# A sparse-attention layer on one core: the output projection's second column half waits for the compressed branch, and the last tile's left half goes first

## The chip, the cores and the metric

The kernel runs on 1 core of a Trainium2 chip. The core has a matrix engine (TensorE, PE in the rows, with its weight loads as PEld), three engines for element-wise work (VectorE or DVE, ScalarE or ACT, GpSimd or POOL) and SyncE (SP), which issues the transfers. Each engine works through its own queue in order, and the engines wait for each other on semaphores. The metric is the device time of the whole program in microseconds (us), as a median over runs. Before the change it is 470.14 us over 3 runs (467.9, 470.14 and 470.22).

## The reference

One layer (DEPTH = 1, so the retention mixer never runs) over 512 tokens of width 1024:

```python
u = rms_norm(h, pre_norm_gain)
q, kv, g, z = split_cols(u @ w_in, ...)       # 16 heads of 64, 4 key/value groups
o_cmp, p_cmp = nsa_compressed(q, kc, vc, table)   # 31 compressed blocks
o_slc = nsa_selected(q, k_s, v_s, sel, table)
o_win = nsa_window(q, k_w, v_w, table)
y = sum(gates * [o_cmp, o_slc, o_win] * silu(z))  # 512 x 1024
out = h + rms_norm(y @ w_out, post_norm_gain)
```

The change touches only the last line: the product with `w_out` (1024 x 1024), the norm over the 1024 columns of a token, the multiplication by the norm's weight, and the sum with `h`.

## The kernel before, in words

All products are float32 split in a high and a low part, so that one product is three matmuls (high by high, low by high, high by low). A weight tile arrives by DMA in one of three buffers `wr`; `split_raw` (L106 to L119) makes the high part on ACT (L113, one cast) and the low part on POOL (L118, two subtractions). A buffer is free for the next load when POOL has read it.

Attention runs over 28 units (group, kind, query tile). For each, `qk` makes scores (L591), a minimum on DVE (L603) and the exponential on ACT (L604); `pv`, one unit later, transposes 128x128 blocks on PE (L681), splits them on ACT (`pth`, L684) and DVE (`ptl`, L685), and multiplies by the values (L714, L715). The head outputs are gathered into `y` (L722 to L731) and split again (`split_y`, L802 and L803). For the last group the order of the query tiles is 0, 3, 2, 1, and tile 1 comes last.

Everything else on PE (projections of the coming groups, and at the end the output projection `wout`) is a generator `fill`, from which the loop at L948 to L965 pulls steps in between, as a running cost estimate `clock` says. A scheduler then orders each engine's queue; `tc.keep_in_program_order` pins single instructions.

`wout` works on four token tiles of 128 rows (`turn = [0, 3, 2, 1]`) and two column halves of 512. The inner dimension has four parts of 256 rows (one for each head group): parts 0 to 2 (`w`, with `yhl` of groups 0 to 2) can be multiplied early, part 3 (`w3`, with `y3`) only when the last group is done. Before the change:

- L839 to L849: for each column half, the three weight tiles are loaded, parts 0 to 2 are multiplied in a PSUM bank of the pair `pj`, and ACT copies the sum into `og` (L849). Tile 1's right half is left out here.
- L850 waits in program order for the compressed branch of group 3, then `w3` is loaded for both halves (L852, L853) and the norm's weight `gb`.
- L875 to L905: for each tile and half, part 3 is multiplied in a bank, DVE adds it to `og` (L892), ACT squares and sums (L894), POOL makes the factor `fss` (`rstd`, L88 and L90), POOL multiplies the left half by the norm's weight (L900) and DVE the right one (L901); one tile later `finish` (L871, DVE) makes `og * fss + x` in `xr`, and SP sends it out (L872). For the last tile, tile 1, parts 0 to 2 of the right half are multiplied first (`late`), then part 3 of the left half, then part 3 of the right half into `late`, from which ACT reads directly.

Of the kernel before, what the change touches and what calls it, by code (L numbers as in the profile page):

```python
# [11 lines left out]
F32 = mybir.dt.float32  # L12
F32R = mybir.dt.float32r
AF = mybir.ActivationFunctionType
ALU = mybir.AluOpType
# [4 lines left out]
S = 512  # L20
D = 1024
# [4 lines left out]
NT = S // 128  # L26
# [25 lines left out]
def nsa_layer(ctx: ExitStack, tc: tile.TileContext, x, pre_gain, post_gain, table, w_in, w_out,  # L52
              k_pos, k_w1, k_w2, v_pos, v_w1, v_w2, hot, hot_c, out):
    nc = tc.nc
    V, A, P, T, SP = nc.vector, nc.scalar, nc.gpsimd, nc.tensor, nc.sync
    x = x.rearrange("b s d -> (b s) d")
    out = out.rearrange("b s d -> (b s) d")
# [12 lines left out]
    pj = lambda: bank("pj", 2)  # L70
# [749 lines left out]
    def wout():  # L820
# [4 lines left out]
        def wo_tile(kp, c, home=None):  # L825
            raw = load_raw([((lambda raw: raw.rearrange("p (k a) c -> p k (a c)", k=2)),
                             w_out[kp * 256:(kp + 1) * 256, c * S:(c + 1) * S].rearrange("(k p) c -> p k c", p=128))])
            return [v.rearrange("p (k a) c -> p k (a c)", k=2) for v in split_raw(raw, 4, A, P, home)]

        def wo_mm(p, kp, t, a, b, first, last):  # L830
            ts = slice(t * 128, (t + 1) * 128)
            for kk in range(2):
                yh, yl = yhl[kp][0][:, kk, ts], yhl[kp][1][:, kk, ts]
                T.matmul(p, yh, a[:, kk], start=first and kk == 0, stop=False)  # L834
                T.matmul(p, yl, a[:, kk], start=False, stop=False)  # L835
                T.matmul(p, yh, b[:, kk], start=False, stop=last and kk == 1)  # L836
                yield 650

        for c in range(2):  # L839
            cs = slice(c * S, (c + 1) * S)  # L840
            w = [wo_tile(kp, c) for kp in range(3)]
            yield 0
            for pair in (turn[0:2], turn[2:4 - c]):
                ps_ = [pj() for _ in pair]
                for kp in range(3):
                    for p, t in zip(ps_, pair):
                        yield from wo_mm(p, kp, t, *w[kp], kp == 0, kp == 2)
                for p, t in zip(ps_, pair):
                    A.copy(og[t][:, cs], p)  # L849
        while (3, B_CMP) not in zdone:  # L850
            yield None
        w3 = [wo_tile(3, 0, [keep.tile([128, 4, 256], F32R, name="w3", tag="u", bufs=8) for _ in range(2)]),  # L852
              wo_tile(3, 1, [at.tile([128, 4, 256], F32R, name="w3", tag="zs", bufs=3) for _ in range(2)])]  # L853
        gb = []
# [2 lines left out]
            SP.dma_start(g_, dview(post_gain, i * S, [[0, 128], [1, S]]))  # L857
            gb.append(g_)
        yield 0
        xrs = []  # L860
        for i in range(NT):
            if i < 3:
                t = wp.tile([128, D], F32, name="xr", tag="wr", bufs=3)
                xrs.append([t[:, 0:S], t[:, S:D]])
            else:
                xrs.append([keep.tile([128, S], F32, name="xr", tag="q", bufs=8) for _ in range(2)])

        def finish(t, xr, ss):
            for i in range(2):
                hs = slice(i * S, (i + 1) * S)  # L870
                V.scalar_tensor_tensor(xr[i], og[t][:, hs], ss, xr[i], op0=ALU.mult, op1=ALU.add)  # L871
                SP.dma_start(out[t * 128:(t + 1) * 128, hs], xr[i])  # L872

        prev = None
        for j, t in enumerate(turn):  # L875
            if j == 3:
                late = pj()
                for kp in range(3):
                    yield from wo_mm(late, kp, turn[3], *w[kp], kp == 0, False)
            while len(ready) <= j:  # L880
                yield None
            assert ready[j] == t
            for i in range(2):
                SP.dma_start(xrs[j][i], x[t * 128:(t + 1) * 128, i * S:(i + 1) * S])
            os_ = [og[t][:, i * S:(i + 1) * S] for i in range(2)]
            for i in range(2):
                held = j == 3 and i == 1
                p = late if held else sb() if j >= 2 else pj()
                yield from wo_mm(p, 3, t, *w3[i], not held, True)
                src = p if held else os_[i]  # L890
                if not held:
                    V.tensor_tensor(os_[i], os_[i], p, op=ALU.add)  # L892
                junk = at.tile([128, S], F32, name="junk", tag="lc", bufs=1)
                A.activation(junk, src, AF.Square, scale=1.0 / 32, accum_out=sumsq[:, t, i:i + 1])  # L894
                if j == 3:
                    V.tensor_tensor(os_[i], src, gb[i], op=ALU.mult)
            ss = const.tile([128, 1], F32, name="fss", tag="fss", bufs=4)
            rstd(ss, sumsq[:, t, 0:1], sumsq[:, t, 1:2])
            if j < 3:
                P.tensor_tensor(os_[0], os_[0], gb[0], op=ALU.mult)  # L900
                V.tensor_tensor(os_[1], os_[1], gb[1], op=ALU.mult)  # L901
            if prev is not None:
                finish(*prev)
            prev = t, xrs[j], ss
        finish(*prev)  # L905

    def kproj(g0):
        alloc_kd(g0)
# [95 lines left out]
```

## Time and profile before

| what | value |
|---|---|
| median of 3 runs | 470.14 us |
| the profiled execution, whole | 469.62 us |
| its span from the first to the last instruction | 467.8 us |
| granted TensorE clock, mean | 0.997 |
| PE busy | 451.2 us (96%) |
| DVE busy | 331.6 us (71%) |
| ACT busy | 274.9 us (59%) |
| POOL busy | 188.5 us (40%) |

Times in the rows are from the start of the span. 1.82 us of the execution lie outside the span. A matmul of 512 columns is shown with about 0.4 us, since it is pipelined: the next one starts about 0.23 us after it when nothing is waited for. A bracket at the end of a row is the time that the engine stood idle before it, and what it waited for.

### The profile page before, as it was taken

The numbers are of one execution on the slowest core, as the hardware profiler recorded it, in microseconds if no ns is written. First come the engines' busy times: TensorE is split into PE (matmuls) and PEld (weight loads), VectorE is DVE, ScalarE is ACT, GpSimd is POOL, SyncE is SP. The second block draws the span as 40 slices with busy tenths as digits, with TensorE's granted clock in tenths as the row PEclk, the third lists the DMA queues.
The fourth block names the chain that finished last, engine by engine and source line by source line (L and its number), as shares of the span: only waits on it lengthen the run. The fifth ranks groups of instructions, "written<-read, shape, count | busy, mean of one in ns | idle before, by whom it ended". The sixth has DMA issues, their size and how long they took to land.

```text
span 467.8 us, 6927 instructions
## 1 busy us (share of the span) xinstructions
PE 451.2 (96%) x2330; PEld 374.9 (80%) x2330; DVE 331.6 (71%) x799; ACT 274.9 (59%) x643; POOL 188.5 (40%) x188
## 2 busy tenths in 40 slices
PE   4999999999999999999999999999999999999993
PEld 3897888878888888888888788888878888887872
DVE  5879843852767888768759777786895867466686
ACT  5712232543776677767756867567675666566631
POOL 3423644243134463351563515245433353366242
PEclk9999999999999999999999999999999999999998
DMA  8589375263111331511141413033070211214013
GB/s 274 162 82 248 116 212 157 74 198 89 47 45 54 105 85 22 166 45 47 45 113 46 127 54 91 1 100 103 3 220 17 79 48 43 90 48 156 25 45 135
DMA packets 45501, 44.63 MB, mean 95 GB/s; under 512 B 7751, under 2 KB 38471, under 8 KB 45466
## 3 DMA queue, kind: packets, MB, share of 16 engines
q1 hardware_dynamic: 44424, 44.00, 33.1%
q8 instruction: 18, 0.29, 0.3%
q10 hardware_dynamic: 1042, 0.20, 0.2%
q14 instruction: 17, 0.14, 0.1%
HBM read 41.99 MB, written 2.20 MB: 94 GB/s over the span
## 4 chain that ended last, share of the span: by engine, by line
PE 84%; DVE 7%; ACT 3%; DMA 2%; issue 2%; POOL 1%; SPq 0%; DVEq 0%; POOLq 0%; ACTq 0%
PE ps_pj L146 11%; PE ps_pj L148 11%; PE ps_pj L147 11%; PE ps_s L591 9%; PE ps_t L681 7%; PE ps_o L715 4%; PE ps_o L714 4%; PE ps_pj L247 2%; PE ps_pj L248 2%; PE ps_pj L249 2%; PE ps_pj L834 2%; PE ps_pj L835 2%; PE ps_pj L836 1%; PE ps_s L247 1%; DMA wr<-in_nsa_w_in_dram 1%
## 5 line engine op out<-in xcount | busy, mean ns | idle before, releaser
L118 POOL TENSOR_TENSOR wl<-wr,wh 128x512 fp32r<-128x512 f32 x94 | 122.9, 1327 | 139.5 <-ACT wh L113 123.1
L146 PE MATMUL ps_pj<-uh,wh 128*128 128x512 f32 x240 | 99.0, 412 | 0.0
L148 PE MATMUL ps_pj<-ul,wh 128*128 128x512 f32 x240 | 94.2, 393 | 0.0
L147 PE MATMUL ps_pj<-uh,wl 128*128 128x512 f32 x240 | 94.2, 392 | 0.0
L604 ACT ACTIVATE p<-p,nm 128x512 f32<-128x512 f32 (+3 forms) x128 | 71.6, 560 | 24.3 <-DVE nm L603 23.5
L685 DVE TENSOR_TENSOR ptl<-ps_t,pth 128x512 fp32r<-128x512 f32 x80 | 55.0, 688 | 28.9 <-ACT pth L684 28.4
L113 ACT CAST wh<-wr 128x1024 fp32r<-128x1024 f32 x47 | 49.2, 1047 | 44.6 <-DMA wr<-in_nsa_w_in_dram 24.8
L591 PE MATMUL ps_s<-kd,q 128*128 128x512 f32 (+5 forms) x256 | 63.9, 336 | 0.6 <-DVE zs L699 0.6
L684 ACT CAST pth<-ps_t 128x512 fp32r<-128x512 f32 x80 | 46.3, 580 | 29.0 <-PE ps_t L681 28.4
L148 PEld LDWEIGHTS ps_pj<-ul,wh 128*128 128x128 f32 x240 | 45.1, 188 | 10.1
L591 PEld LDWEIGHTS ps_s<-kd,q 128*128 128x128 f32 x256 | 43.8, 189 | 9.0 <-DVE zs L699 1.1
L146 PEld LDWEIGHTS ps_pj<-uh,wh 128*128 128x128 f32 x240 | 45.2, 188 | 6.1
L147 PEld LDWEIGHTS ps_pj<-uh,wl 128*128 128x128 f32 x240 | 45.3, 189 | 5.9
L603 DVE CUSTOM_DVE_ANT_0 p<-ps_s,bias 128x128 f32<-128x128 f32 (+3 forms) x80 | 34.6, 447 | 20.9 <-PE ps_s L591 20.7
L681 PE MATMUL ps_t<-ident,p 128*128 128x128 f32 x320 | 48.4, 272 | 0.0
L681 PEld LDWEIGHTS ps_t<-ident,p 128*128 128x128 f32 x320 | 39.7, 140 | 9.3
L714 PE MATMUL ps_o<-pth,vt 128*128 128x512 f32 x80 | 33.7, 421 | 0.4 <-ACT pth L684 0.4
L728 POOL TENSOR_TENSOR y<-otmp,zs 128x256 f32<-128x256 f32 x16 | 12.3, 772 | 51.5 <-DVE otmp L725 51.5
L603 DVE CUSTOM_DVE_ANT_1 p<-ps_s,bias 128x256 f32<-128x256 f32 (+2 forms) x48 | 26.3, 554 | 9.1 <-PE ps_s L591 8.6
L715 PE MATMUL ps_o<-ptl,vt 128*128 128x512 f32 x80 | 32.3, 404 | 0.4 <-DVE ptl L685 0.2
L730 POOL TENSOR_TENSOR otmp<-otmp,zs 128x256 f32<-128x256 f32 x15 | 11.1, 741 | 38.3 <-DVE otmp L725 38.3
L569 ACT ACTIVATE zs<-ps_pj 128x512 f32<-128x512 f32 x22 | 13.1, 596 | 19.5 <-PE ps_pj L148 19.4
(268 smaller groups left out, 899.6 us busy)
## 6 DMA issues: line engine op xcount, KB each, us to landing
wr<-in_nsa_w_in_dram SPq DMA_DIRECT2D x36, 512.0 KB
wr<-in_nsa_w_in_dram SPq DMA_DIRECT2D x16, 256.0 KB
bias<-toepd SPq DMA_DIRECT2D x16, 256.0 KB
wr<-in_nsa_w_out_dram SPq DMA_DIRECT2D x8, 512.0 KB
xt<-in_x_dram SPq DMA_DIRECT2D x4, 512.0 KB
wr<-in_nsa_cmp_k_w_dram SPq DMA_DIRECT2D x4, 512.0 KB
wr<-in_nsa_cmp_v_w_dram SPq DMA_DIRECT2D x4, 512.0 KB
xr<-in_x_dram SPq DMA_DIRECT2D x8, 256.0 KB
```

The costliest lines, as they stand in the source:

```text
L113: A.copy(h[:, 0:kn], raw[:, 0:kn])
L118: el.tensor_tensor(l[:, ks], raw[:, ks], h[:, ks].bitcast(F32), op=ALU.subtract)
L146: T.matmul(p, a, rh, start=k == 0, stop=False)
L147: T.matmul(p, b, rh, start=False, stop=False)
L148: T.matmul(p, a, rl, start=False, stop=k == KT - 1)
L591: T.matmul(po, qs[h][:, qt * 128:(qt + 1) * 128], kds[h // R][:, i, c0:c0 + n], start=i == 0, stop=i == 1)
L603: V.tensor_tensor_reduce(pd, src, bi, 1.0, BIG, ALU.add, ALU.min, st["nm"][:, hh:hh + 1])
L604: A.activation(po, po, AF.Exp, bias=st["nm"][:, hh:hh + 1], scale=-1.0, accum_out=st["rs"][:, hh:hh + 1])
L681: T.transpose(tp[:, hh * 128:(hh + 1) * 128], st["p"][hh][:, c:c + 128], ident)
L685: V.tensor_tensor(pl, tp, ph.bitcast(F32), op=ALU.subtract)
L714: T.matmul(acc, v, ph, start=j == 0, stop=False)
L715: T.matmul(acc, v, pl, start=False, stop=j == qt)
```

## The change

- The three weight tiles of the second column half are asked for after the wait for the compressed branch, together with `w3`, so their products stand later in program order.
- Tile 0's right half is not copied into `og` any more. Its bank stays open (`held`) until part 3 is added in the same bank, and ACT and DVE read the sum there.
- The product with the norm's weight is on DVE for both halves (L922); POOL's L900 is gone.
- For tile 1, part 3 of the left half is multiplied before the eighteen matmuls of parts 0 to 2 of the right half, and tile 2's finishing steps stand on DVE after the left half's product, pinned in program order. Its products go to a new tile `og3`.
- `xr` is allocated inside the loop; its loads are the same.

```diff
-        for c in range(2):
-            cs = slice(c * S, (c + 1) * S)
-            w = [wo_tile(kp, c) for kp in range(3)]
-            yield 0
-            for pair in (turn[0:2], turn[2:4 - c]):
-                ps_ = [pj() for _ in pair]
-                for kp in range(3):
-                    for p, t in zip(ps_, pair):
-                        yield from wo_mm(p, kp, t, *w[kp], kp == 0, kp == 2)
-                for p, t in zip(ps_, pair):
-                    A.copy(og[t][:, cs], p)
+        def half(t, c):
+            return og[t][:, c * S:(c + 1) * S]
+
+        def partial(w, c, ts):
+            ps_ = [pj() for _ in ts]
+            for kp in range(3):
+                for p, t in zip(ps_, ts):
+                    yield from wo_mm(p, kp, t, *w[kp], kp == 0, kp == 2 and (c, t) != (1, turn[0]))
+            for p, t in zip(ps_, ts):
+                if (c, t) == (1, turn[0]):
+                    held.append(p)
+                else:
+                    A.copy(half(t, c), p)
+
+        held = []
+        w = [wo_tile(kp, 0) for kp in range(3)]
+        yield 0
+        yield from partial(w, 0, turn[0:2])
+        yield from partial(w, 0, turn[2:4])
         while (3, B_CMP) not in zdone:
             yield None
+        w = [wo_tile(kp, 1) for kp in range(3)]
...
+        def last(i):
+            return tc.keep_in_program_order(i)
+
+        def finish(t, xr, ss, i):
+            a = V.scalar_tensor_tensor(xr[i], g3[i] if t == turn[3] else half(t, i), ss, xr[i], op0=ALU.mult, op1=ALU.add)
+            if t in turn[2:]:
+                last(a)
+            SP.dma_start(out[t * 128:(t + 1) * 128, i * S:(i + 1) * S], xr[i])
...
-            if j == 3:
-                late = pj()
-                for kp in range(3):
-                    yield from wo_mm(late, kp, turn[3], *w[kp], kp == 0, False)
+            if j < 3:
+                if j == 0:
+                    yield from partial(w, 1, turn[0:2])
+                if j == 1:
+                    yield from partial(w, 1, turn[2:3])
...
+                whole = i == 1 and j in (0, 3)
+                if whole and j == 3:
+                    held.append(pj())
+                    for kp in range(3):
+                        yield from wo_mm(held[-1], kp, t, *w[kp], kp == 0, False)
+                p = held.pop(0) if whole else sb() if j >= 2 else pj()
+                yield from wo_mm(p, 3, t, *w3[i], not whole, True)
+                if not whole:
+                    a = V.tensor_tensor(half(t, i), half(t, i), p, op=ALU.add)
...
                 if j == 3:
-                    V.tensor_tensor(os_[i], src, gb[i], op=ALU.mult)
+                    g3.append(at.tile([128, S], F32, name="og3", tag="p", bufs=8))
+                    last(V.tensor_tensor(g3[i], src[i], gb[i], op=ALU.mult))
+                    if i == 0:
+                        finish(*prev, 0)
+                        finish(*prev, 1)
             rstd(ss, sumsq[:, t, 0:1], sumsq[:, t, 1:2])
             if j < 3:
-                P.tensor_tensor(os_[0], os_[0], gb[0], op=ALU.mult)
-                V.tensor_tensor(os_[1], os_[1], gb[1], op=ALU.mult)
+                for i in range(2):
+                    V.tensor_tensor(half(t, i), src[i], gb[i], op=ALU.mult)
...
```

ACT's queue where the weights for part 3 are cast, before. `w3_4917` belongs to the right half and to the second of the two loads (`wr_4919`), `w3_4910` to the left half and the first load (`wr_4912`); `pth_4698` and `pth_4722` are the casts that the attention of the unit before last waits for.

```order
L849 COPY og_4409<-ps_pj_4539 128x512
L802 CAST y30_4689<-y_4184 128x2x128
L113 CAST w3_4917<-wr_4919 128x1024
L684 CAST pth_4698<-ps_t_4693 128x512
L604 ACTIVATE p_4684,rs_4588<-p_4684,nm_4587 128x384
L113 CAST w3_4910<-wr_4912 128x1024
L684 CAST pth_4722<-ps_t_4717 128x512
```

The same place now. `w3_4694` is the first load (`wr_4696`), `w3_4701` the second (`wr_4703`).

```order
L851 COPY og_4409<-ps_pj_4539 128x512
L802 CAST y30_4660<-y_4184 128x2x128
L604 ACTIVATE p_4655,rs_4588<-p_4655,nm_4587 128x384
L684 CAST pth_4669<-ps_t_4664 128x512
L113 CAST w3_4694<-wr_4696 128x1024
L113 CAST w3_4701<-wr_4703 128x1024
L684 CAST pth_4740<-ps_t_4735 128x512
```

The exponential and one cast of the attention moved ahead of both casts of `w3`, and these two changed places. SP's queue keeps its order of loads; the one that is cast second now is also the one that is loaded second. On PE the two matmuls L591 and the four transposes L681 that feed this exponential and this cast moved up past six matmuls of the output projection, and on DVE the minimum L603 moved up past L803.

DVE's queue at the end of the program, before. Tile 3 is `og_4411`, tile 2 is `og_4410`, tile 1, the last, is `og_4409`.

```order
L871 SCALAR_TENSOR_TENSOR xr_4929<-og_4411,fss_4982,xr_4929 128x512 x2
L901 TENSOR_TENSOR og_4410<-og_4410,pgain_4926 128x512
L871 SCALAR_TENSOR_TENSOR xr_4930<-og_4410,fss_5013,xr_4930 128x512 x2
L892 TENSOR_TENSOR og_4409<-og_4409,ps_s_5043 128x512
L896 TENSOR_TENSOR og_4409<-og_4409,pgain_4924 128x512
L896 TENSOR_TENSOR og_4409<-ps_pj_5022,pgain_4926 128x512
L871 SCALAR_TENSOR_TENSOR xr_4931<-og_4409,fss_5063,xr_4931 128x512
L871 SCALAR_TENSOR_TENSOR xr_4932<-og_4409,fss_5063,xr_4932 128x512
```

The same place now.

```order
L922 TENSOR_TENSOR og_4410<-og_4410,pgain_4708 128x512
L874 SCALAR_TENSOR_TENSOR xr_4953<-og_4411,fss_4956,xr_4953 128x512
L922 TENSOR_TENSOR og_4410<-og_4410,pgain_4710 128x512
L907 TENSOR_TENSOR og_4409<-og_4409,ps_s_5022 128x512
L915 TENSOR_TENSOR og3_5032<-og_4409,pgain_4708 128x512
L874 SCALAR_TENSOR_TENSOR xr_4985<-og_4410,fss_4988,xr_4985 128x512 x2
L915 TENSOR_TENSOR og3_5065<-ps_pj_5038,pgain_4710 128x512
L874 SCALAR_TENSOR_TENSOR xr_5017<-og3_5032,fss_5021,xr_5017 128x512
L874 SCALAR_TENSOR_TENSOR xr_5018<-og3_5065,fss_5021,xr_5018 128x512
```

The last tile's left half is added (L892, now L907) and multiplied ahead of tile 2's two finishing steps instead of behind them, and left-half products stand here that were POOL's.

DVE's queue where the last `y` is made, now (tile 0 is `og_4408`; L730, L731 and L803 make tile 1's `y` and its low part).

```order
L922 TENSOR_TENSOR og_4408<-ps_pj_4712,pgain_4710 128x512
L730 TENSOR_TENSOR otmp_4909<-otmp_4909,zs_4228 128x256
L874 SCALAR_TENSOR_TENSOR xr_4869<-og_4408,fss_4872,xr_4869 128x512
L731 TENSOR_TENSOR y_4184<-y_4184,otmp_4909 128x2x128
L874 SCALAR_TENSOR_TENSOR xr_4869<-og_4408,fss_4872,xr_4869 128x512
L803 TENSOR_TENSOR y31_4661<-y_4184,y30_4660 128x2x128
```

Before, L730, L731 and L803 followed each other here; now tile 0's product and its two finishing steps, which wait for POOL's `fss_4872`, stand between them.

## Rows read from the trace of the kernel before

**Rows 1.** The page's busy times of the engines.

```profile
PE 451.2 (96%) x2330; PEld 374.9 (80%) x2330; DVE 331.6 (71%) x799; ACT 274.9 (59%) x643; POOL 188.5 (40%) x188
```

**Rows 2.** Stretches: length, busy of PE, PEld, DVE, ACT, POOL, clock, DMA, GB/s.

```profile
417.40:419.60 2.20, 2.20 (x12) 1.85 (x11) 1.21 (x3) 1.41 (x2) 1.30 (x2) 1.00 0.58 218
...
425.69:429.89 4.20, 3.47 (x21) 2.51 (x20) 3.79 (x7) 2.85 (x6) 4.20 (x4) 1.00 0.47 156
453.40:460.40 7.00, 7.00 (x31) 5.43 (x29) 7.00 (x11) 2.17 (x6) 4.01 (x5) 1.00 0.40 150
```

**Rows 3.** ACT in order of time: start, duration, instruction, [idle before, releaser].

```profile
422.40 0.41 ACT L802 CAST y<-y 128x256 fp32r<-128x256 f32 x1
424.49 1.05 ACT L113 CAST w<-wr 128x1024 fp32r<-128x1024 f32 x1 [1.68 <-DMA wr<-in_nsa_w_out_dram]
425.44 0.58 ACT L684 CAST pth<-ps_t 128x512 fp32r<-128x512 f32 x1
425.92 0.62 ACT L604 ACTIVATE p<-p,nm 128x384 f32<-128x384 f32 x1
...
427.47 1.07 ACT L684 CAST pth<-ps_t 128x512 fp32r<-128x512 f32 x2
430.17 0.59 ACT L684 CAST pth<-ps_t 128x512 fp32r<-128x512 f32 x1 [1.63 <-PE ps_t L681]
```

**Rows 4.** PE in order of time in the same stretch.

```profile
425.69 0.60 PE L681 MATMUL ps_t<-ident,p 128*128 128x128 f32 x4
...
426.81 0.50 PE L715 MATMUL ps_o<-ptl,vt 128*128 128x512 f32 x1 [0.22 <-DVE ptl L685]
...
429.54 0.60 PE L681 MATMUL ps_t<-ident,p 128*128 128x128 f32 x4
429.89 0.48 PE L834 MATMUL ps_pj<-wh,yhl 128*128 128x512 f32 x1
```

**Rows 5.** DVE in order of time in the same stretch.

```profile
421.19 0.69 DVE L787 TENSOR_TENSOR y<-y,ctmp 128x512 f32<-128x512 f32 x1
...
426.06 0.69 DVE L685 TENSOR_TENSOR ptl<-ps_t,pth 128x512 fp32r<-128x512 f32 x1 [1.91 <-ACT pth L684]
...
426.88 1.55 DVE L650 TENSOR_TENSOR f<-f,gate 128x256 f32<-128x256 f32 x1
428.35 0.68 DVE L685 TENSOR_TENSOR ptl<-ps_t,pth 128x512 fp32r<-128x512 f32 x1
```

**Rows 6.** All engines in order of time, the end of the program.

```profile
460.01 0.39 PE L836 MATMUL ps_pj<-w,y 128*128 128x512 f32 x1
460.23 0.67 DVE L892 TENSOR_TENSOR og<-og,ps_s 128x512 f32<-128x512 f32 x1
...
460.99 0.63 ACT L894 ACTIVATE junk<-og 128x512 f32<-128x512 f32 x1 [4.12 <-DVE og L892]
...
461.75 0.60 ACT L894 ACTIVATE junk<-ps_pj 128x512 f32<-128x512 f32 x1
...
462.24 0.19 ACT L894 ACTIVATION_READ_ACCUMULATOR junk<-ps_pj 128x1 f32 x1
...
463.51 1.42 DVE L871 SCALAR_TENSOR_TENSOR xr<-og,fss,xr 128x512 f32<-128x512 f32 x2 [0.35 <-POOL fss L90]
```

**Rows 7.** Tile `og` from 440 to 468: duration ns min/median/max, first and last start.

```profile
L871 DVE SCALAR_TENSOR_TENSOR xr<-og,fss,xr x8: 739/746/1772, 451.2 to 464.2; 128x512 f32<-128x512 f32 x8
L900 POOL TENSOR_TENSOR og<-og,pgain x3: 1285/1289/1293, 448.6 to 455.9; 128x512 f32<-128x512 f32 x3
L901 DVE TENSOR_TENSOR og<-og,pgain x3: 679/680/685, 450.1 to 458.3; 128x512 f32<-128x512 f32 x3
```

**Rows 8.** DVE and POOL in order of time, where tiles are finished.

```profile
451.17 1.28 POOL L900 TENSOR_TENSOR og<-og,pgain 128x512 f32<-128x512 f32 x1
451.23 1.77 DVE L871 SCALAR_TENSOR_TENSOR xr<-og,fss,xr 128x512 f32<-128x512 f32 x1 [0.46 <-POOL fss L90]
...
455.98 2.39 DVE L871 SCALAR_TENSOR_TENSOR xr<-og,fss,xr 128x512 f32<-128x512 f32 x2
```

More of the change, by code (lines that the diff above doesn't have):

```diff
@@ L859, in wout @@
         yield 0
[L860 to L874, printed above, removed]
-        for j, t in enumerate(turn):
-            if j == 3:
-                late = pj()
-                for kp in range(3):
-                    yield from wo_mm(late, kp, turn[3], *w[kp], kp == 0, False)
+        def last(i):
[5 more added lines that the diff above has]
+            SP.dma_start(out[t * 128:(t + 1) * 128, i * S:(i + 1) * S], xr[i])
+        prev, g3 = None, []
+        for j, t in enumerate(turn):
+            if j < 3:
[3 more added lines that the diff above has]
+                    yield from partial(w, 1, turn[2:3])
             while len(ready) <= j:
@@ L882, in wout @@
             assert ready[j] == t
+            if j < 3:
+                x_ = wp.tile([128, D], F32, name="xr", tag="wr", bufs=3)
+                xr = [x_[:, 0:S], x_[:, S:D]]
+            else:
+                xr = [keep.tile([128, S], F32, name="xr", tag="q", bufs=8) for _ in range(2)]
             for i in range(2):
-                SP.dma_start(xrs[j][i], x[t * 128:(t + 1) * 128, i * S:(i + 1) * S])
-            os_ = [og[t][:, i * S:(i + 1) * S] for i in range(2)]
+                SP.dma_start(xr[i], x[t * 128:(t + 1) * 128, i * S:(i + 1) * S])
@@ L886, in wout @@
+            ss = const.tile([128, 1], F32, name="fss", tag="fss", bufs=4)
+            src = []
             for i in range(2):
[L887 to L892, printed above, removed]
+                whole = i == 1 and j in (0, 3)
[7 more added lines that the diff above has]
+                    a = V.tensor_tensor(half(t, i), half(t, i), p, op=ALU.add)
+                    if j == 3:
+                        last(a)
+                src.append(p if whole else half(t, i))
@@ L893, in wout @@
                 junk = at.tile([128, S], F32, name="junk", tag="lc", bufs=1)
-                A.activation(junk, src, AF.Square, scale=1.0 / 32, accum_out=sumsq[:, t, i:i + 1])
+                A.activation(junk, src[i], AF.Square, scale=1.0 / 32, accum_out=sumsq[:, t, i:i + 1])
                 if j == 3:
-                    V.tensor_tensor(os_[i], src, gb[i], op=ALU.mult)
-            ss = const.tile([128, 1], F32, name="fss", tag="fss", bufs=4)
+                    g3.append(at.tile([128, S], F32, name="og3", tag="p", bufs=8))
[3 more added lines that the diff above has]
+                        finish(*prev, 1)
@@ L898, in wout @@
             rstd(ss, sumsq[:, t, 0:1], sumsq[:, t, 1:2])
             if j < 3:
-                P.tensor_tensor(os_[0], os_[0], gb[0], op=ALU.mult)
-                V.tensor_tensor(os_[1], os_[1], gb[1], op=ALU.mult)
[L902 to L905, printed above, removed]
+                for i in range(2):
+                    V.tensor_tensor(half(t, i), src[i], gb[i], op=ALU.mult)
+                if prev is not None:
+                    for i in range(2):
+                        finish(*prev, i)
@@ L907, in kproj @@
+            prev = t, xr, ss
+        for i in range(2):
+            finish(*prev, i)
     def kproj(g0):
```

## The prediction

> **What bounds the kernel now.** The page's busy times come first: PE is busy for 451.2 of the 467.8 us of the span, the next engine, DVE, for 331.6 [rows 1]. So a change of order pays in two places only: where PE stands still while work is left, and in the tail, after PE's last matmul. The number of matmuls is the same before and after, and their clock is 1.00 in every stretch shown with matmuls in it [rows 2], so PE's own work is not a term. I then read the timeline for these two places.
>
> The first is 425.69 to 429.89, the one stretch near the change where PE is busy for only 3.47 of 4.20 us [rows 2]. ACT shows why: after L802 (422.40, 0.41 long) it stood 1.68 us for the transfer of a `w3` tile and cast it at 424.49. Behind that in its queue were the attention's cast L684, which started at 425.44, and the exponential L604 [rows 3]. DVE's L685 had to wait for the first of them until 426.06 [rows 5], and PE's L715 for that until 426.81 [rows 4]. A second round of the same ended with DVE's L685 at 428.35 + 0.68 = 429.03 [rows 5], and the next matmul of the output projection came at 429.89 [rows 4].
>
> The second place is the tail. PE's last matmul starts at 460.01 and ends at 460.40. But DVE was in tile 2's finishing steps and added the left half of tile 1 only at 460.23; ACT squared this half at 460.99 and the right half, complete in PSUM since 460.40, only at 461.75. Its sum was read by 462.24 + 0.19 = 462.43, and DVE's finishing steps began at 463.51 [rows 6]. The span ends 467.80 - 463.51 = 4.29 us after that: two steps of 1.42 us together, the last transfer and the program's end.
>
> **The change part by part.**
>
> *ACT's order at the `w3` casts.* In the changed queue the exponential and one L684 stand ahead of both `w3` casts. I follow the queue with before's durations. L604 needs DVE's minimum, which now comes directly after L787, at 421.19 + 0.69 = 421.88 [rows 5]; the matmuls for it moved up past six others, so it is ready at about 422.5. ACT is free at 422.81 (L802). L604: 0.62, to 423.43; L684: 0.48 to the next start (425.44 to 425.92 [rows 3]), 423.91. The first `w3` cast takes 0.95 to the next start (424.49 to 425.44 [rows 3]), 424.86. Its load is there: the DMA engines moved 218 GB/s in 417.40 to 419.60 [rows 2], 480 KB, nearly all of one 512 KB tile. The second cast needs the second load, which landed at 424.49 in the trace and stands at the same place of SP's queue, behind the same POOL step; it is there with 0.37 us to spare. The cast ends its slot at 425.81. The next L684 waits for PE's transposes, unmoved at 425.69 + 0.60 = 426.29, and starts 0.03 after them, as at 430.17 after 429.54 + 0.60 [rows 3, 4]: 426.32. So ACT is no longer late. DVE's L685 follows 0.62 after such a cast starts (425.44 to 426.06) and takes 0.69: it ends at 427.63. In the trace the L685 at this place of the program ended at 429.03, after which PE reached the output projection 0.86 us later. **PE gains 429.03 - 427.63 = 1.40 us.**
>
> Bounds: if the transfer or the minimum came late, up to all of it goes, 0. The most is what PE lost there: with 12 transposes at 0.35 for four (429.54 to 429.89), four matmuls of 0.23, and 0.4 for two short groups, 4.20 us hold some 2.4 us of work, so 1.8 us. I take 1.40. Part of DVE's delay in the trace is its L650 at 426.88, which took 1.55 us beside POOL's steps [rows 5]; now it stands earlier, and even if it takes 1.55 there, the L685 behind it is done before PE asks for it at 426.3.
>
> *The same gain further on.* PE is in its own order after 429.89 and DVE, ACT and POOL follow it, so the 1.40 us stay, if nothing new makes PE wait. One place is near: the right half of tile 3 goes into the bank that ACT must first copy out (tile 2's right half). That copy stands on ACT behind a cast of the last `y`, which waits for DVE's L731, which now stands behind a finishing step of tile 0, which waits for POOL's factor. Following these queues from 1.40 us earlier, with ACT's extra square of 0.73, I get the bank free at about 447.8, when PE wants it at 447.7. A wait of this kind costs about 0.2 us. Before, PE had one of that size at the same place for DVE's L892. So net 0; the bounds are -0.2 and +1.4, the latter if a finishing step takes its longest, 1.77 in place of 0.74 [rows 7], and the factor 0.4 more.
>
> *Left half first, and finishing steps moved.* Tile 1's left half is complete eighteen matmuls earlier and is added, squared and multiplied before PE's end; at PE's end E only the right half is left. ACT's square starts 0.04 after E, the sum is read 462.43 - 461.75 = 0.68 later, and the finishing steps come 463.51 - 462.43 = 1.08 after that [rows 6]: E + 1.80. The trace had 463.51 - 460.40 = E + 3.11. **The tail gains 1.31 us.** Its cover is DVE: the left half, two products and tile 2's finishing must be done by then. By the same walk DVE ends tile 2's steps at about 458.2; with E = 459.0 the last product may start as late as E + 1.1, so there are about 1.9 us to spare. If that cover is gone, each us beyond it costs one.
>
> *Products on DVE.* Three of 0.68 on DVE in place of three of 1.29 on POOL, and one L892 of 0.67 less: 1.37 us more work on DVE. In 453.40 to 460.40 DVE was busy all 7.00 us [rows 2], so this is not obviously free. But that time holds blocked steps: a finishing step took 1.77 at 451.23 while POOL ran L900 at 451.17, and the pair at 455.98 took 2.39, against 0.74 for one [rows 7, 8]. That is 1.03 + 0.91 = 1.94 us that goes if L900 does it. I cost the products at 0, hidden behind PE's matmuls up to E; bounds 0 and +1.37.
>
> The Trainium skill, Perfetto Trace Analysis, section Optimizing Scalar/DVE Operations, speaks against this part: it says that work may be moved off VectorE, even to GpSimd, where VectorE is saturated, and adds that between these two a move might not help, since they share an SBUF read port. By its first half the sum would lose the 1.37 us; by the second, which the 1.77 beside L900 fits, it would not. I go by the rows.
>
> *The rest at nothing.* Tile 0's right half is no longer copied by ACT (about 0.6 us, hidden by PE either way). `xr`'s loads and the new tile `og3` add no instruction; SP's queue keeps its order of loads and stores.
>
> **Sum.** 1.40 + 0 + 1.31 = 2.7 us off the profiled execution's 469.62: 466.9. That execution is 0.5 us below the median of 470.14, inside the spread of 467.9 to 470.22; I say 467.0.
>
> **Rivals.**
>
> *PE gains nothing.* Its wait comes back a few us later, or the second load arrives over 0.9 us later than 424.49. For it: ACT has two casts in a row now, 2 x 0.95 us ahead of an L684. Against: the queues give room. Time: 469.62 - 1.31 = 468.3.
>
> *The bank.* Tile 0's finishing steps hold up ACT's copy, and PE waits 1.4 us at tile 3. For it: steps of 1.77 are in the trace. Against: POOL has no long step left there. Time: 469.62 - 2.7 + 1.4 = 468.3.
>
> *DVE becomes the bound, and the kernel slower.* The place is DVE's queue from 453.40 to PE's end, full in the trace. If the long finishing steps do not come from L900 but stay, the queue gets 1.37 us longer and the last finishing steps move by that: 469.62 + 1.37 = 471.0. This is what the rule on a saturated VectorE amounts to here. It decides once DVE ends tile 2's second step more than 1.9 + 2.7 us later than I reckon. Against it: blocked steps are only those beside L900.
>
> *No change.* The two gains were bounded by something else that ends at the same time, such as the stores; 469.6. Against: the last store is issued after the last step.
>
> **How the numbers follow.** My forecast 0.58, with its own range 465.8 to 467.8 (PE's gain up to 1.8 and the 0.2 of the old wait; or 0.9 less); no gain on PE 0.20; the bank 0.12; slower 0.06; none 0.04. The range reaches both cases at 468.3 with 1 us for the spread of runs: 465.2 to 469.4. About 0.5%, 2.35 us, can be told from no change. The forecast lies only 0.35 beyond it, so a good fifth of its chance falls within; of the two cases at 468.3 a fifth falls beyond. That gives 0.46 + 0.07 = 0.53 faster, 0.42 the same and 0.05 slower.
>
> **What would show it.** On ACT, a `w3` cast at 424 to 425 with no 1.68 us wait before it, and the exponential before 423.5. On PE, the matmuls after the stretch at 428.5 and the last one ending near 459.0. After it, ACT's square at once, the finishing steps 1.8 us later, and none of them over 0.8 us. I am wrong if PE ends at 460 or later, if a matmul of tile 3 waits for ACT's copy by over half a us, or if DVE is still in tile 2's steps when ACT squares.

## The result, and the profile after

The changed kernel takes 467.0 us (median of 8 runs, 465.29 to 468.0); the kernel before took 469.6 us in runs beside it. The ratio is 0.9944, 95% interval 0.9925 to 0.9963: 2.6 us, or 0.56%, faster. The prediction said 467.0. The profiled execution took 466.85 us with a span of 465.0 (before 469.62 and 467.8).

The page's busy times, against [rows 1], hardly differ; the span is shorter because the gaps are.

```profile
PE 450.9 (97%) x2330; PEld 375.3 (81%) x2330; DVE 330.6 (71%) x801; ACT 274.3 (59%) x642; POOL 184.7 (40%) x185
```

The first place is the stretch of [rows 2]. From the four transposes at 425.69 to the next matmul of the output projection took 4.20 us, 3.47 of them busy. It now takes 428.45 - 425.58 = 2.87 us, and PE is busy throughout (columns as in [rows 2]). The second line is the end of the program up to PE's last matmul; DVE, full there before, now has 0.62 us to spare.

```profile
425.69:428.50 2.81, 2.81 (x22) 2.41 (x20) 1.53 (x3) 1.17 (x2) 2.81 (x3) 1.00 0.53 187
453.40:458.85 5.45, 5.45 (x24) 4.16 (x22) 4.83 (x8) 1.45 (x4) 1.60 (x2) 1.00 0.32 123
```

ACT in order of time answers to [rows 3]. The exponential L604 and a cast L684 stand ahead of both `w3` casts (L113), which follow each other with no wait for a transfer. The next L684 waits for PE's transposes, not PE for it.

```profile
422.60 0.61 ACT L604 ACTIVATE p<-p,nm 128x384 f32<-128x384 f32 x1
...
423.21 0.57 ACT L684 CAST pth<-ps_t 128x512 fp32r<-128x512 f32 x1
423.68 2.01 ACT L113 CAST w<-wr 128x1024 fp32r<-128x1024 f32 x2
426.27 0.59 ACT L684 CAST pth<-ps_t 128x512 fp32r<-128x512 f32 x1 [0.58 <-PE ps_t L681]
427.12 0.59 ACT L684 CAST pth<-ps_t 128x512 fp32r<-128x512 f32 x1 [0.27 <-PE ps_t L681]
```

The tail, all engines in order of time, answers to [rows 6]. When PE's last matmul ends at 458.46 + 0.39 = 458.85, ACT squares the right half 0.10 us later, with no other square ahead of it. The finishing steps start at 460.72.

```profile
456.86 1.41 DVE L874 SCALAR_TENSOR_TENSOR xr<-og,fss,xr 128x512 f32<-128x512 f32 x2
...
458.46 0.39 PE L836 MATMUL ps_pj<-w,y 128*128 128x512 f32 x1
458.95 0.60 ACT L912 ACTIVATE junk<-ps_pj 128x512 f32<-128x512 f32 x1 [1.92 <-PE ps_pj L836]
459.44 0.19 ACT L912 ACTIVATION_READ_ACCUMULATOR junk<-ps_pj 128x1 f32 x1
459.67 0.69 DVE L915 TENSOR_TENSOR og<-ps_pj,pgain 128x512 f32<-128x512 f32 x1 [1.40 <-ACT junk L912]
...
460.72 1.42 DVE L874 SCALAR_TENSOR_TENSOR xr<-og,fss,xr 128x512 f32<-128x512 f32 x2 [0.35 <-POOL fss L90]
```

By the durations of tile `og` (minimum, median and maximum in ns), no finishing step is stretched any more; the longest in [rows 7] was 1772.

```profile
L874 DVE SCALAR_TENSOR_TENSOR xr<-og,fss,xr x8: 743/746/753, 445.4 to 461.4; 128x512 f32<-128x512 f32 x8
```

To compare profiles, I measure from one common event. PE's last L782, a matmul of the compressed branch, starts at 419.57 us before and at 419.46 after, ahead of the change's first effect on PE's order (420.85 after). In the profiles below it lies anywhere from 418.36 to 420.91. From its start to the start of PE's last matmul tells what PE gained; from that matmul's end, 0.39 later, to the first of the two final finishing steps is the tail.

```
kernel                        L782 to the   tail   L782 to the   by the trace   by the timed
                              last matmul           final step   vs before us   ratio us
before                           40.44      3.11      43.94          -              -
after                            39.00      1.87      41.26        -2.68          -2.6
left half first alone            41.93      1.86      44.18        +0.24          -0.2
order alone                      39.12      3.11      42.62        -1.32          -1.6
after, products on POOL          38.99      1.86      41.24        -2.70          -2.8
after, tile 0 copied             39.28      1.86      41.53        -2.41          -2.8
before, w3 loads swapped         39.41      3.09      42.89        -1.05          -0.8
after, six more on DVE           38.99      3.67      43.05        -0.89          -1.1
left half, products on DVE       40.41      1.86      42.66        -1.28          -1.1
order and left half              40.64      1.86      42.89        -1.05          -1.4
left half, six ahead             40.98      1.86      43.23        -0.71          -0.9
order, left half, six ahead      39.49      1.85      41.73        -2.21          -2.2
```

All of the change's 2.68 us is thus 1.44 on PE and 1.24 in the tail. The last column is the ratio less one, times the 469.6 to 470.0 us of the kernel before; its intervals are given with each run and reach 0.7 to 1.1 us to either side.

### The profile page after: what moved, and what is told of

The parts are those of the page before. It is cut to its first block, busy times and chain, and to the rows that moved or that the text cites. A ratio compares the mean times of both kernels' runs of the same rounds, so it can differ in the third digit from the quotient of the medians.

```text
span 465.0 us, 6924 instructions
## 1 busy us (share of the span) xinstructions
PE 450.9 (97%) x2330; PEld 375.3 (81%) x2330; DVE 330.6 (71%) x801; ACT 274.3 (59%) x642; POOL 184.7 (40%) x185
## 4 chain that ended last, share of the span: by engine, by line
PE 89%; DVE 4%; ACT 3%; issue 2%; POOL 1%; DVEq 0%; POOLq 0%; ACTq 0%
PE ps_pj L146 11%; PE ps_pj L148 11%; PE ps_pj L147 11%; PE ps_s L591 9%; PE ps_t L681 7%; PE ps_o L715 4%; PE ps_o L714 4%; PE ps_pj L834 3%; PE ps_pj L835 3%; PE ps_pj L836 3%; PE ps_s L247 2%; PE ps_s L248 2%; PE ps_s L249 2%; PE ps_pj L247 2%; PE ps_pj L248 1%
## 5 line engine op out<-in xcount | busy, mean ns | idle before, releaser
L604 ACT ACTIVATE p<-p,nm 128x512 f32<-128x512 f32 (+3 forms) x128 | 71.6, 560 | 24.3 <-DVE nm L603 23.5
L113 ACT CAST wh<-wr 128x1024 fp32r<-128x1024 f32 x47 | 49.2, 1047 | 43.5 <-DMA wr<-in_nsa_w_in_dram 20.1
L591 PE MATMUL ps_s<-kd,q 128*128 128x512 f32 (+5 forms) x256 | 63.9, 336 | 0.7 <-DVE zs L699 0.6
L684 ACT CAST pth<-ps_t 128x512 fp32r<-128x512 f32 x80 | 46.4, 580 | 29.3 <-PE ps_t L681 28.7
L591 PEld LDWEIGHTS ps_s<-kd,q 128*128 128x128 f32 x256 | 43.9, 189 | 9.0 <-DVE zs L699 1.2
L603 DVE CUSTOM_DVE_ANT_0 p<-ps_s,bias 128x128 f32<-128x128 f32 (+3 forms) x80 | 34.6, 447 | 20.7 <-PE ps_s L591 20.5
L681 PE MATMUL ps_t<-ident,p 128*128 128x128 f32 x320 | 48.4, 272 | 0.0
L681 PEld LDWEIGHTS ps_t<-ident,p 128*128 128x128 f32 x320 | 39.7, 140 | 9.4
L603 DVE CUSTOM_DVE_ANT_1 p<-ps_s,bias 128x256 f32<-128x256 f32 (+2 forms) x48 | 26.3, 555 | 9.3 <-PE ps_s L591 8.6
L730 POOL TENSOR_TENSOR otmp<-otmp,zs 128x256 f32<-128x256 f32 x15 | 11.1, 741 | 37.9 <-DVE otmp L725 37.9
```

The costliest lines, as they stand in the source:

```text
L113: A.copy(h[:, 0:kn], raw[:, 0:kn])
L591: T.matmul(po, qs[h][:, qt * 128:(qt + 1) * 128], kds[h // R][:, i, c0:c0 + n], start=i == 0, stop=i == 1)
L603: V.tensor_tensor_reduce(pd, src, bi, 1.0, BIG, ALU.add, ALU.min, st["nm"][:, hh:hh + 1])
L604: A.activation(po, po, AF.Exp, bias=st["nm"][:, hh:hh + 1], scale=-1.0, accum_out=st["rs"][:, hh:hh + 1])
L681: T.transpose(tp[:, hh * 128:(hh + 1) * 128], st["p"][hh][:, c:c + 128], ident)
```

## The experiments

**Left half first, alone.** The last tile's left half and the moved finishing steps, in the kernel before. Its core:

```diff
-            if j == 3:
-                late = pj()
-                for kp in range(3):
-                    yield from wo_mm(late, kp, turn[3], *w[kp], kp == 0, False)
...
                 held = j == 3 and i == 1
+                if held:
+                    late = pj()
+                    for kp in range(3):
+                        yield from wo_mm(late, kp, turn[3], *w[kp], kp == 0, False)
...
+                    if i == 0:
+                        finish(*prev)
```

> The kernel before with only the tail of the change: the last tile's left half ahead of the eighteen matmuls of the right half, tile 2's finishing steps pinned behind it; the weights' order and POOL's products as before. My theory (two gains that add up): PE's last matmul ends where it did, at 460.4, with the stretch at 425.7 to 429.9 as slow as it was; the finishing steps begin 1.8 to 1.9 us after it in place of 3.1, so the span is 1.2 us shorter, ratio 0.997. Rival (DVE bounds the end while POOL makes products beside it): tile 2's finishing steps last past ACT's square, and 0.5 us or less is gained, ratio 0.999.

Measured 469.39 us, ratio 0.9995 [0.998, 1.001]. The total is what the rival gave. But the tail is 1.86 us, as the theory had it, and DVE is not its bound. The gain is lost earlier, in a wait of PE. All engines in order of time:

```profile
449.92 1.28 POOL L909 TENSOR_TENSOR og<-og,pgain 128x512 f32<-128x512 f32 x1
449.98 1.77 DVE L873 SCALAR_TENSOR_TENSOR xr<-og,fss,xr 128x512 f32<-128x512 f32 x1 [0.46 <-POOL fss L90]
...
451.68 0.67 DVE L896 TENSOR_TENSOR og<-og,ps_pj 128x512 f32<-128x512 f32 x1
...
452.11 0.39 PE L834 MATMUL ps_pj<-wh,yhl 128*128 128x512 f32 x1
452.28 0.74 DVE L873 SCALAR_TENSOR_TENSOR xr<-og,fss,xr 128x512 f32<-128x512 f32 x1
...
452.94 0.68 DVE L896 TENSOR_TENSOR og<-og,ps_s 128x512 f32<-128x512 f32 x1
...
453.76 0.47 PE L834 MATMUL ps_s<-w,y 128*128 128x512 f32 x1 [1.26 <-DVE og L896]
```

PE's L834 at 453.76 is the first matmul of the last tile's left half. It needs the bank `ps_s` that DVE's addition of tile 2's left half frees at 452.94 + 0.68 = 453.62, and that addition stands behind tile 0's two finishing steps. In the kernel before, the last tile's eighteen `late` matmuls stood between the two uses of the bank, some 4.1 us of PE's work. Here the scheduler puts one there. By starts the wait costs more than the 1.26 us listed: from that one (452.11) to L834 1.65 us pass, and from L834 to the next matmul 0.31, where 0.23 is usual both times; that is 1.50 us in all, and the table's 41.93 - 40.44 agrees to 0.01. So the 1.25 us gained in the tail are spent on PE. Neither theory had this.

**Order alone.** The right half's loads and matmuls move behind the wait for the compressed branch; nothing else.

```diff
-        for c in range(2):
+        def parts(c):
...
-            w = [wo_tile(kp, c) for kp in range(3)]
-            yield 0
...
+        yield from parts(0)
         while (3, B_CMP) not in zdone:
             yield None
+        w = [wo_tile(kp, 1) for kp in range(3)]
...
         yield 0
+        yield from parts(1)
```

> The kernel before with only the first part of the change: the weights of the second column half asked for after the wait for the compressed branch; tile 0 is copied, POOL makes left products and the tail stands as before. ACT's queue gets the order of the changed kernel. My theory: ACT does not wait for the transfer, PE reaches the output projection after the stretch 1.3 to 1.4 us earlier and everything after follows, so the span is 1.3 us shorter, ratio 0.997. Rival (the chain that ended before's program ran over DVE, not over PE's last matmuls): PE ends 1.3 us earlier and the program does not, ratio 1.000.

Measured 468.26 us, ratio 0.9967 [0.9951, 0.9983]: the theory. The wait for the transfer is gone from ACT, as in the changed kernel, and the tail is before's, 3.11 us.

```profile
422.17 0.62 ACT L604 ACTIVATE p<-p,nm 128x384 f32<-128x384 f32 x1
...
422.78 0.57 ACT L684 CAST pth<-ps_t 128x512 fp32r<-128x512 f32 x1
423.25 2.00 ACT L113 CAST w<-wr 128x1024 fp32r<-128x1024 f32 x2
```

**The changed kernel with one product of each tile back on POOL.**

```diff
-                    V.tensor_tensor(half(t, i), src[i], gb[i], op=ALU.mult)
+                    (V if i else P).tensor_tensor(half(t, i), src[i], gb[i], op=ALU.mult)
```

> The changed kernel with the three left-half products back on POOL, nothing else moved on PE and ACT. My theory: DVE has some 1.8 us to spare before the last product, so finishing steps of 1.5 to 1.8 us come back beside POOL's products and the time does not move: within 0.3 us of the changed kernel, ratio to before 0.994 to 0.995. Rival (the products had to leave POOL for the gain): the steps' extra 1.9 us shows at the end, by 1 us or more, ratio 0.997.

Measured 467.59 us, ratio 0.994 [0.9916, 0.9963], as the whole change. The stretched step is back beside POOL's product, and nothing waits for it: tile 2's left half had been added before it (452.09, 0.69 us).

```profile
452.09 0.69 DVE L907 TENSOR_TENSOR og<-og,ps_s 128x512 f32<-128x512 f32 x1 [0.67 <-PE ps_s L836]
...
453.78 1.28 POOL L922 TENSOR_TENSOR og<-og,pgain 128x512 f32<-128x512 f32 x1
453.84 1.77 DVE L874 SCALAR_TENSOR_TENSOR xr<-og,fss,xr 128x512 f32<-128x512 f32 x1 [0.46 <-POOL fss L90]
```

**The changed kernel with tile 0's right half copied and added, as before.**

```diff
-                if (c, t) == (1, turn[0]):
-                    held.append(p)
-                else:
-                    A.copy(half(t, c), p)
+                A.copy(half(t, c), p)
...
-                whole = i == 1 and j in (0, 3)
+                whole = i == 1 and j == 3
```

> The changed kernel with tile 0's right half copied by ACT and added by DVE, as before, in place of the held bank. My theory: one ACT copy of 0.6 us and one DVE addition of 0.7 us are hidden by PE: no difference over 0.2 us from the changed kernel, ratio to before 0.994. Rival (the held bank matters for PE's two pj banks): a matmul waits for the copy, 0.5 us or more.

Measured 467.48 us, ratio 0.9941 [0.9923, 0.9959]: worth nothing that the times show. The table has PE 0.28 us longer than after, within the interval; 0.25 of it is at the start of the last tile's left half, where the matmuls start at 452.24, 452.62 and 452.95 and the usual step is 0.23.

**The kernel before with `w3`'s halves loaded in the other order.** This leaves PE's and DVE's orders alone and moves one `w3` cast on ACT, with its two subtractions on POOL.

```diff
-        w3 = [wo_tile(3, 0, [keep.tile([128, 4, 256], F32R, name="w3", tag="u", bufs=8) for _ in range(2)]),
-              wo_tile(3, 1, [at.tile([128, 4, 256], F32R, name="w3", tag="zs", bufs=3) for _ in range(2)])]
+        w3 = [wo_tile(3, 1, [at.tile([128, 4, 256], F32R, name="w3", tag="zs", bufs=3) for _ in range(2)]),
+              wo_tile(3, 0, [keep.tile([128, 4, 256], F32R, name="w3", tag="u", bufs=8) for _ in range(2)])][::-1]
```

> The kernel before, with one edit: the two halves of w3 are loaded in the opposite order. The instruction order of TensorE, VectorE, GpSimd and the DMA queue stays that of the kernel before; on ScalarE one of the two w3 casts moves ahead of the copy, the y cast and the waiting cast, so one cast of 1.04 us no longer stands behind the wait for the transfer. Theory (ScalarE's in-order queue behind that wait sets the pace of TensorE there): the later pair of pth casts, at 427.47 us before, starts about 0.95 us earlier, TensorE leaves the stretch about 0.9 us earlier, and the run is 0.9 us shorter, ratio 0.998; the wait of 1.68 us itself stays. Rival (it is TensorE's own order, the moved right-half products, that closed the idle gaps, and ScalarE's queue was a bystander): TensorE's own order is untouched, so ratio 1.000. A third way: the early cast now waits for its own transfer ahead of the copy, and the run is up to 0.5 us slower.

Measured 469.08 us, ratio 0.9983 [0.9962, 1.0005]. By time alone it can't be told from no change. The trace can: from the first L684 behind the wait to the second took 427.47 - 425.44 = 2.03 us [rows 3], and takes 1.18 here; PE's last matmul comes 1.03 us earlier by the table. So, by the trace, ACT's queue is enough for 1.03 of the 1.44 us without PE's own new order. The wait for the transfer itself stays here; whether the rest is that wait or PE's order isn't shown.

```profile
425.05 1.05 ACT L113 CAST w<-wr 128x1024 fp32r<-128x1024 f32 x1 [1.10 <-DMA wr<-in_nsa_w_out_dram]
426.01 0.58 ACT L684 CAST pth<-ps_t 128x512 fp32r<-128x512 f32 x1
426.48 0.62 ACT L604 ACTIVATE p<-p,nm 128x384 f32<-128x384 f32 x1
...
427.19 0.59 ACT L684 CAST pth<-ps_t 128x512 fp32r<-128x512 f32 x1
```

**The changed kernel with six more products on DVE**, ahead of tile 2's finishing steps; their results are not used.

```diff
                     if i == 0:
+                        for _ in range(6):
+                            more = at.tile([128, S], F32, name="more", tag="p", bufs=8)
+                            last(V.tensor_tensor(more, g3[0], gb[0], op=ALU.mult))
```

> The changed kernel with six more VectorE products of 128x512 (results unused) between the last tile's left-half weight product and the third tile's two finishing steps; about 0.6 us each when back to back, 3.7 us in all. Theory (VectorE has slack at the end: in the changed kernel its queue is empty from 458.27 us to 459.67 us, 1.4 us, and the last weight product waits for ScalarE, the final steps for GpSimd's factor): the first 1.4 us and the 0.4 us that the last steps wait for the factor are hidden, so the end is about 1.9 us later, ratio to the kernel before about 0.998. Rival (the saturated look of VectorE before was real, it is the bound of the end): all 3.7 us show, ratio 1.002. If the products were hidden entirely, 0.994.

Measured 468.61 us, ratio 0.9977 [0.9958, 0.9997]: the theory's 0.998. The six take 3.70 us, and the final steps start 462.84 - 459.17 = 3.67 us after PE's end in place of 1.87. So 3.70 - 1.80 = 1.9 us are hidden, the slack that the prediction worked out.

```profile
457.29 3.70 DVE L919 TENSOR_TENSOR more<-og,pgain 128x512 f32<-128x512 f32 x6
...
458.78 0.39 PE L836 MATMUL ps_pj<-w,y 128*128 128x512 f32 x1
...
462.24 0.68 DVE L915 TENSOR_TENSOR og<-ps_pj,pgain 128x512 f32<-128x512 f32 x1
462.84 1.40 DVE L874 SCALAR_TENSOR_TENSOR xr<-og,fss,xr 128x512 f32<-128x512 f32 x2
```

**Left half first, with the products on DVE.** The first experiment's kernel with one edit.

```diff
-                P.tensor_tensor(os_[0], os_[0], gb[0], op=ALU.mult)
+                V.tensor_tensor(os_[0], os_[0], gb[0], op=ALU.mult)
```

> The tail-only kernel (old order ahead of it, the last tile's left half first) with all weight products on VectorE instead of GpSimd. Theory: the tail alone gained nothing because TensorE waits 1.26 us at 453.8 us for the bank that VectorE's addition of the third tile's left half frees, and that addition is late behind GpSimd's products (1.29 us each ahead of the factor, and the finishing step beside them takes 1.77 us instead of 0.74 us). With the products on VectorE that wait falls to 0.3 us or less and the tail's 1.2 us stand: ratio 0.9975. Rival (the wait is a matter of the bank order alone, whoever computes the products): ratio 0.9995 as for the tail alone. Second rival (VectorE's queue, now with three more products of 0.7 us ahead of that addition, is later still): wait over 1.3 us, ratio 1.000 or above.

Measured 468.91 us, ratio 0.9977 [0.9958, 0.9996], as the theory. PE's wait is gone: over 448 to 457 us PE is busy 9.00 of 9.00 us, where the left half alone had 7.74 (first line; the second is this run).

```profile
448.00:457.00 9.00, 7.74 (x34) 6.08 (x33) 8.31 (x10) 3.01 (x10) 6.49 (x9) 1.00 0.15 58
...
448.00:457.00 9.00, 9.00 (x40) 7.39 (x40) 8.64 (x14) 4.33 (x12) 3.16 (x5) 1.00 0.17 64
```

But it went mostly for another reason than I gave. The addition of tile 2's left half starts at 454.04, 6.61 us ahead of PE's end at 460.65. The left half alone, without its 1.50 us, would have it 460.68 - 1.50 - 452.94 = 6.24 us ahead. So it is 0.4 us earlier, of 1.5 needed. The rest is PE's order: the scheduler now puts six of the last tile's right-half matmuls ahead of its left half, in place of one, 5 x 0.23 = 1.15 us more.

**Order and left half, without the other parts.** The edits of the first two experiments together.

> The two parts that carry time, alone: the right half waits for the compressed branch, and the last tile's left half comes first; the first tile is not completed in its bank, and one weight product of each tile stays on GpSimd. If the parts add up, as the prediction summed them: ratio 0.994, as the whole change. Theory from the tail-only run (without either the early first tile or the products on VectorE, VectorE's addition of the third tile's left half comes late and TensorE waits for its bank): the order's 1.4 us stand, a wait of 0.8 to 1.3 us eats the tail's gain, ratio 0.9965.

Measured 468.44 us, ratio 0.9971 [0.9952, 0.9991]: the parts do not add up. The same wait is there, listed as 1.24 us, and PE takes 1.52 us longer than with the order alone.

```profile
452.37 0.67 DVE L900 TENSOR_TENSOR og<-og,ps_s 128x512 f32<-128x512 f32 x1
...
453.19 0.47 PE L834 MATMUL ps_s<-w,y 128*128 128x512 f32 x1 [1.24 <-DVE og L900]
```

This run leaves out more than the held bank and the products on DVE. In the changed kernel the eighteen early matmuls of tile 2's right half (`wh,yhl` in the rows) also stand behind tile 0's part 3 (`w,y`): the diff asks for them at `j == 1`, which the list of the change does not name. Here, as in the kernel before, they stand ahead of it. The first two rows are the changed kernel, the last two this run.

```profile
441.98 0.39 PE L836 MATMUL ps_pj<-w,y 128*128 128x512 f32 x1
442.21 0.40 PE L834 MATMUL ps_pj<-wh,yhl 128*128 128x512 f32 x1
...
442.87 0.39 PE L836 MATMUL ps_pj<-wl,yhl 128*128 128x512 f32 x1
443.10 0.39 PE L834 MATMUL ps_pj<-w,y 128*128 128x512 f32 x1
```

The runs with the products on POOL and with tile 0 copied both keep the changed kernel's place. What it does can be read from the time between the end of PE's work on tile 2's left half and DVE's addition of it: 0.04 us in the changed kernel and with the products on POOL, 0.62 with tile 0 copied, 1.65 in the left half with the products on DVE, 2.00 here and 2.03 in the kernel before. From 1.65 to 0.62 it is this place that differs, and the loads' order, which alone moves nothing here (2.03). So about 1.0 of the 2.0 us seems to come from this place. With it and the held bank the products can be on either engine; no run moves it alone.

**Left half first, six matmuls ahead.** To settle it, the one edit that differs on PE: the last tile's first six right-half matmuls are written ahead of its left half. Products stay on POOL.

```diff
-                if held:
-                    late = pj()
-                    for kp in range(3):
+                if j == 3:
+                    if not held:
+                        late = pj()
+                    for kp in (range(1, 3) if held else range(1)):
```

> The tail-only kernel with one edit: six of the last tile's eighteen right-half matmuls, which need no new bank, stand ahead of its left half instead of one. Nothing moves on VectorE, ScalarE, GpSimd or the DMA queue; the weight products stay as they were. Theory (the tail's gain is eaten by TensorE's wait of 1.26 us for the bank that the addition of the third tile's left half frees, and the tail with VectorE products differed in TensorE's order, not in when that addition came): five matmuls of 0.23 us cover 1.15 us of that wait, it falls to 0.1 us, the run is 1.1 us shorter than the tail-only one, ratio 0.9975. Rival (VectorE, with GpSimd's products beside it, is late itself and sets the end): the wait only moves on, ratio 0.9995 as for the tail alone.

Measured 468.62 us, ratio 0.9981 [0.9964, 0.9998]. The addition comes as in the left half alone, the wait is nearly gone (8.92 of 9.00 us busy), and by the table 0.95 of PE's 1.50 us are back. By time alone this run and the left half alone can't be told apart, since their intervals overlap.

```profile
448.00:457.00 9.00, 8.92 (x39) 7.03 (x38) 7.62 (x9) 3.62 (x10) 6.57 (x8) 1.00 0.15 58
```

Its DVE has no slack left, though: tile 2's steps end as the last product may start.

```profile
459.66 1.41 DVE L873 SCALAR_TENSOR_TENSOR xr<-og,fss,xr 128x512 f32<-128x512 f32 x2
...
461.03 0.69 DVE L904 TENSOR_TENSOR og<-ps_pj,pgain 128x512 f32<-128x512 f32 x1
```

**Order and left half, six matmuls ahead.** The same edit on the kernel with the order.

> Order and tail alone (no early first tile, one product of each tile on GpSimd) with the same edit: six right-half matmuls of the last tile ahead of its left half instead of one. Theory: the wait of 1.24 us at 453.19 us falls to 0.1 us and the whole change's gain is there with neither of its two other parts: ratio 0.9943. Rival (those parts are needed because VectorE's chain is late): ratio 0.997 as without the edit.

Measured 467.73 us, ratio 0.9954 [0.9938, 0.9969]; 0.9943 lies inside, 0.997 just outside. With neither the early first tile nor the products on DVE, 2.2 of the 2.6 us are there. No version was faster than the changed kernel by more than its interval.

## Why the prediction was right

*ACT's order* was put at 1.40 us. PE gained 1.44 in the changed kernel and 1.32 with the order alone; the stretch itself became 4.20 - 2.87 = 1.33 shorter. The walk through the queue held: exponential at 422.60, reckoned 422.5 to 422.81; first `w3` cast at 423.68, 0.23 us before the time reckoned; the L684 at 426.27, reckoned 426.32. The second load came before its cast was due. Swapping the loads shows that ACT's queue behind the transfer cost at least 1.03 us of it.

*Left half first* was put at 1.31 us and measured 3.11 - 1.87 = 1.24 us. Nearly all of the missing 0.07 is ACT's start, 0.10 after PE's end and not 0.04, a figure that no row of the prediction shows. The slack of 1.9 us on DVE was right to 0.1 us.

*Products on DVE, cost 0; the rest at nothing.* Right for the changed kernel: the products can go back to POOL, and tile 0 can be copied, each alone and with no loss that the times show. But the tail's gain needs a cover that the sum did not list. With only the order and the left half the kernel loses 1.2 us of the whole gain by the timed ratios, 1.6 by the traces. The reason is a wait. The prediction moved the eighteen matmuls behind the last tile's left half and did not ask what they had covered there, which was the bank `ps_s`, 1.5 us. In the changed kernel it is covered because tile 0 is finished at 445.35 to 447.10, ahead of those additions. That takes tile 2's early matmuls behind tile 0's last ones on PE, as well as the held bank; the runs do not separate the two fully. The prediction looked for a new wait of PE at tile 3 alone. That its two gains add up is therefore in part luck: it counted on no cover at tile 2, and the changed kernel has one.

*The bank at tile 3* was put at a net 0. ACT copied it at 446.78 + 0.58 = 447.36, PE wanted it at 447.73, and before's wait of 0.2 us went. A wait of the size of the rival of that name, 1.5 us for its 1.4, does exist, but not in the changed kernel, and at another bank: it is for tile 2's addition by DVE, not for tile 3's copy by ACT.

*DVE as the bound* fell. The Trainium skill, Perfetto Trace Analysis, section Optimizing Scalar/DVE Operations, says that moving work away from a saturated VectorE may make sense. DVE was at 7.00 of 7.00 us here, yet 1.37 us more work on it cost nothing that the times show. Of that busy time 1.94 us were steps stretched beside POOL's products, and they are gone. With the products back on POOL, one step took 1.77 us again and the kernel was as fast, so it is the slack at the end that decides. The section's own caveat, that a move between VectorE and GpSimd might not help because they share a read port, fits the stretched steps; the rows show the stretching, not the port.

*The range.* Its lower end, 465.8, does not come out of the terms given for it: 466.9 less 0.4 and 0.2 is 466.3. Nothing above rests on it.

## What to carry to other kernels

Before matmuls are moved, list for each of them which bank or buffer it gave time to be freed, not only whom it feeds; the cost of losing that cover can equal the gain. An engine with an in-order queue that waits for a transfer holds up everything behind it, so put first what others wait for. And when parts of a change are taken back, compare the engines' queues for what else goes with them: here the place of eighteen matmuls, which no list named, went too.

## What the runs showed of the hardware

POOL's smallest instructions are stretched beside some of DVE's, as DVE's finishing steps were beside POOL's products (1.77 us, against 0.74 for one alone [rows 7, 8]). In the changed kernel the 128x1 step L88 took 1.04 us beside a finishing step and a product on DVE, against 0.30 at the end of the program, where DVE ran L915, which reads one of its inputs from PSUM. Nothing waited for the longer one.

```profile
454.27 0.75 DVE L874 SCALAR_TENSOR_TENSOR xr<-og,fss,xr 128x512 f32<-128x512 f32 x1
...
454.67 1.04 POOL L88 TENSOR_SCALAR fss<-sumsq 128x1 f32<-128x1 f32 x1 [2.30 <-ACT junk L912]
454.93 0.68 DVE L922 TENSOR_TENSOR og<-og,pgain 128x512 f32<-128x512 f32 x1
...
459.67 0.69 DVE L915 TENSOR_TENSOR og<-ps_pj,pgain 128x512 f32<-128x512 f32 x1 [1.40 <-ACT junk L912]
459.73 0.30 POOL L88 TENSOR_SCALAR fss<-sumsq 128x1 f32<-128x1 f32 x1 [3.39 <-ACT junk L912]
```

A single profile's span can't rank kernels as close as these. PE's last L782, ahead of the change's first effect, scattered over 2.55 us between profiles. The left half alone had a span of 466.9 us, 0.9 below before's, with the same timed median within its interval; measured from L782 it was 0.24 us slower.
